# A planner that counts the delay of an engine's own last result, in a hybrid layer on one core

## The chip, the cores and the metric

The kernel runs on one core of a Trainium2 chip. Its time is the device time of one execution, in microseconds (us). The work is divided among five instruction streams, each of which runs in the order in which it was written: TensorE (PE) does the matmuls, VectorE (DVE), ScalarE (ACT) and GpSimd (POOL) the elementwise work, and SyncE (SP) issues the DMA transfers. An engine that meets an instruction whose input is not ready stands still, and all that is written behind that instruction waits with it.

## The reference

One layer over 1024 prompt tokens and 8 sample tokens, model width 1024, all in float32. Cut to what matters:

```python
xn   = rmsnorm(h, pre_g)
u, v, z_a, x_b, z_b, g_a, g_b = split(xn @ w_in)      # w_in: 1024 x 7168
u, vn = gelu(u), layernorm(gelu(v))
y_a  = u * (tril(w_s) mixes each 128-token chunk of vn, + b_s) * silu(z_a)
y_b  = blockdiag_linear(mean over 2/4/8/16 trailing rows of x_b, - x_b) * scale * silu(z_b)
m    = sigmoid(g_a) * (y_a @ w_pa) + sigmoid(g_b) * (y_b @ w_pb)
h    = h + rmsnorm(m @ w_out, post_g)
e    = p @ w_ple
h    = h + rmsnorm(sigmoid(rmsnorm(h, ple_in_g) @ w_pg) * e, ple_out_g)
```

The outputs are h for the prompt and the samples, the last chunk of vn, and the pooling rows (the last 15 rows of x_b, and for the samples the state shifted by one).

## The kernel before, in words

**Products.** Each float32 operand is cut into a high and a low part of the matmul type float32r, and a product is three matmuls (high by high, high by low, low by high). The high part is a copy on ACT (`xbw<-xbs`), the low part a subtraction on DVE (`xbw<-xbs,xbw`). Each large product is made by seven block products instead of eight (Strassen), so that sums and differences of blocks have to be made on DVE: of weight blocks (`xbs<-big`, `wgraw<-wgraw`), of token blocks (`big<-big`), and of results in PSUM (`acc<-acc,w`, `one<-acc,w`). The names of the PSUM banks are `acc00`, `acc01`, `acc10`, `acc11`, `one0`, `one1` (the views of the profile leave the digits out), and two more are used in turn for the rest (`q`, `mix`, `accm`, `sps`, `state`). There are 6013 matmuls, of 512 columns (`one`) or 260 (`acc`) for the most part.

**Stages.** The stages follow each other on PE: `p @ w_ple` with the first blocks of v; v; g_a with the mixing of the chunks; u and z_a in pairs of block products; x_b and z_b with the pooling; g_b; the two products with w_pa and w_pb; w_out; and at the end the gate w_pg. Between the stages tensors are parked in DRAM: `ya<-za` is the store of y_a rows, `big<-ya` their way back, `big<-mix` the way back of the mixed chunks, `wg<-wgraw` the parking of scaled columns of w_pg, `wolow<-big` that of block sums of w_out. `big` is the operand of the running stage and also the place where weights land (`big<-in_w_in_dram`). Everything else in SBUF lies in 46 equal slots, which are given to tensors one after the other (`SLOTS`), so that a tensor's first writer also waits for the last user of its slot.

**What sets the order.** The code does not write the order of the work. Every operation is recorded by the class `Planner` as an `Op`, with its readers and writers, and when all are recorded `Planner.order` simulates the five streams with durations out of a small model (`duration`), and at each step issues the operation that can start first; among those that can start at the same time the one with the smallest due time (`late`, counted back from the matmuls that need it, shifted by `PUSH`). When an operation's end is known, its successors get the time from which they can start (`ready`): on another engine that is the end plus `SEEN`, on the same engine the end itself. The list that comes out is written to the engines by `play`; all instructions carry therefore one line number, L408. The planner's times are used for nothing else: on the chip every instruction starts when its semaphores allow it. `order` also gives the slots, in the order of issue.

The constants that the change touches: `PUSH["out"]` and `PUSH["tok"]` move the due times of the work that takes a finished block product out of PSUM (`pushed("out" if form.tail else "tok", evacuate, p)`), `HASTE` is the number of microseconds within which the norms between w_out and the gate are to be done (`hasty`), and `TURNS` names for each pair of token blocks the steps at which the output norm (`out_finish`), the sum for the next norm (`gate_norm`) and the transposing of its result (`gate_input`) are recorded.

## Time and profile before

| | |
|---|---|
| median of 3 runs | 979.25 us (978.5 to 979.53) |
| the profiled execution | 978.55 us |
| its span, first to last instruction | 976.8 us |
| granted TensorE clock | 0.996 |
| PE busy | 960.1 us (98%), 6013 matmuls |
| DVE busy | 788.1 us (81%), 1326 instructions |
| ACT busy | 535.0 us (55%) |
| POOL busy | 76.8 us (8%) |
| DMA | 194.23 MB, mean 199 GB/s |

A row of the timeline has the start in us from the beginning of the span, the length, the engine, the line, the operation, out<-in by the program's names, the shapes, the count of instructions merged into it, and, where the engine stood idle before it, how long and what released it. Names have lost their numbers there: `za` may be any of za#0 to za#7. A row of the waits has the waiting instruction, what it waited for, the sum in us, how often, and the longest.

### The profile page before, as it was taken

The page shows a single profiled execution, that of the slowest core. Times are in us where ns is not written, and L with a number is a line of the kernel's source. Part 1 is how long each engine was busy: PE and PEld are TensorE (multiplying, and loading weights), DVE is VectorE, ACT ScalarE, POOL GpSimd, SP SyncE. Part 2 cuts the span into 40 slices and gives each one's busy share as a digit, 9 for nine tenths or more (in the row PEclk, how much of TensorE's full clock was granted, in tenths as well). Part 3 has the DMA queues.
Part 4 walks back from the last instruction along what each step waited for, and adds up shares of the span by engine and source line. Part 5 has one row for each costly group of instructions (what it writes and reads, how often), then busy time and mean ns, then how long its engine had stood idle before and what let it go on. Part 6 is the DMA issues. An engine that isn't in the chain of part 4 may idle for free.

```text
span 976.8 us, 16155 instructions
## 1 busy us (share of the span) xinstructions
PE 960.1 (98%) x6013; PEld 852.2 (87%) x6013; DVE 788.1 (81%) x1326; ACT 535.0 (55%) x1041; POOL 76.8 (8%) x117
## 2 busy tenths in 40 slices
PE   9999999999999999999999999999999999999995
PEld 7889999999998899899999999999999987688765
DVE  6998559988587978879698986596599789699957
ACT  7765457767444554344455443572363284688744
POOL 3200000000000000001011200000000001221203
PEclk9999999999999999999999999999999999999998
DMA  9524975554358945654344485793573276699795
GB/s 339 178 87 86 192 180 186 158 176 130 109 202 257 327 162 198 227 161 143 119 162 138 152 287 198 276 335 105 193 285 113 108 280 196 159 306 345 202 324 175
DMA packets 137982, 194.23 MB, mean 199 GB/s; under 512 B 42407, under 2 KB 93647, under 8 KB 137894
## 3 DMA queue, kind: packets, MB, share of 16 engines
q1 hardware_dynamic: 135853, 185.82, 57.4%
q0 software_dynamic: 2048, 7.37, 4.2%
q8 instruction: 47, 0.77, 0.3%
q14 instruction: 34, 0.27, 0.1%
HBM read 133.46 MB, written 60.16 MB: 198 GB/s over the span
## 4 chain that ended last, share of the span: by engine, by line
PE 88%; DMA 5%; DVE 4%; issue 1%; ACT 1%; POOL 1%; SPq 0%; POOLq 0%; DVEq 0%; ACTq 0%
PE acc L408 47%; PE one L408 36%; PE mix L408 1%; DVE big L408 1%; PE accm L408 1%; PE sps L408 1%; DVE za L408 1%; DMA big<-in_w_in_dram 1%; DMA wgraw<-in_w_pg_dram 1%; DMA big<-in_state_pool_dram 1%; DVE ge L408 1%; DMA weraw<-in_w_ple_dram 1%; POOL rstd L408 1%; DMA big<-in_w_out_dram 1%; DMA wohigh<-big 1%
## 5 line engine op out<-in xcount | busy, mean ns | idle before, releaser
L408 POOL TENSOR_TENSOR rstd<-ms,mhalf 128x1 f32<-128x1 f32 (+1 forms) x37 | 33.9, 928 | 504.2 <-DVE ms L408 475.1
L408 DVE TENSOR_TENSOR big<-big 128x512 f32<-128x512 f32 (+7 forms) x80 | 58.6, 741 | 4.7 <-DMA big<-in_w_in_dram 2.4
L408 DVE TENSOR_TENSOR one<-acc,w 128x260 f32<-128x260 f32 (+1 forms) x68 | 29.3, 431 | 21.6 <-PE acc L408 17.5
L408 ACT ACTIVATE qh<-big 128x512 fp32r<-128x512 f32 (+2 forms) x32 | 21.8, 696 | 30.5 <-DVE big L408 23.6
L408 ACT ACTIVATE acc<-one 128x260 f32<-128x260 f32 x66 | 21.3, 366 | 30.7 <-PE one L408 30.7
L408 ACT ACTIVATE w<-acc 128x260 f32<-128x260 f32 (+1 forms) x66 | 25.1, 410 | 21.5 <-PE acc L408 21.3
L408 DVE TENSOR_TENSOR ql<-big,qh 128x512 fp32r<-128x512 f32 (+2 forms) x32 | 24.3, 771 | 9.5 <-PE one L408 3.5
L408 POOL COPY big<-xb 128x1 f32<-128x1 f32 x8 | 4.5, 558 | 260.4 <-DMA yalow<-za 188.9
L408 ACT ACTIVATE gbw<-gbs 128x512 fp32r<-128x512 f32 x16 | 10.0, 628 | 21.1 <-DVE gbs L408 15.3
L408 ACT ACTIVATE pbw<-pbs 128x512 fp32r<-128x512 f32 x16 | 9.9, 627 | 18.1 <-DVE pbs L408 14.2
L408 DVE TENSOR_TENSOR gbw<-gbs,gbw 128x512 fp32r<-128x512 f32 x16 | 11.0, 687 | 10.9 <-ACT gbw L408 10.9
L408 ACT ACTIVATE paw<-pas 128x512 fp32r<-128x512 f32 x16 | 10.0, 628 | 13.3 <-DVE pas L408 11.2
L408 POOL COPY big<-big 128x2 f32<-128x2 f32 (+2 forms) x12 | 12.6, 1048 | 53.4 <-DVE big L408 39.1
L408 ACT ACTIVATE big<-mix 128x256 f32<-128x256 f32 x32 | 12.0, 382 | 8.4 <-PE mix L408 7.9
L408 ACT ACTIVATE junk<-h 128x512 bf16<-128x512 f32 x20 | 12.6, 630 | 6.6 <-DMA h<-in_x_prompt_dram 3.8
L408 ACT ACTIVATE vw<-vs 128x512 fp32r<-128x512 f32 x16 | 10.0, 626 | 10.6 <-DVE vs L408 7.9
L408 PE MATMUL mix<-wst,vh 128*128 128x256 f32 x64 | 15.6, 319 | 0.0
L408 DVE TENSOR_TENSOR za<-za,big 128x1024 f32<-128x1024 f32 (+2 forms) x16 | 15.2, 956 | 0.2
L408 ACT ACTIVATE junk<-ge 128x512 bf16<-128x512 f32 (+2 forms) x19 | 11.5, 603 | 6.9 <-DVE ge L408 6.1
L408 DVE TENSOR_TENSOR za<-za,u 128x1032 f32<-128x1032 f32 x8 | 9.8, 1229 | 6.3 <-ACT za L408 6.3
L408 ACT ACTIVATE acc<-none 128x8 f32<-128x8 f32 x33 | 5.9, 179 | 16.3 <-DVE big L408 7.8
L408 ACT ACT_TABLE_LOAD x11 | 14.1, 1283 | 1.0 <-PEq L2133 0.8
(712 smaller groups left out, 3635.1 us busy)
## 6 DMA issues: line engine op xcount, KB each, us to landing
big<-in_w_in_dram SPq DMA_DIRECT2D x48, 512.0 KB
ga<-ga SPq DMA_DIRECT2D x16, 516.0 KB
gb<-gb SPq DMA_DIRECT2D x16, 516.0 KB
ya<-za SPq DMA_DIRECT2D x8, 516.0 KB
yb<-zb SPq DMA_DIRECT2D x8, 516.0 KB
x<-in_x_prompt_dram SPq DMA_DIRECT2D x8, 512.0 KB
vraw<-in_w_in_dram SPq DMA_DIRECT2D x8, 512.0 KB
e<-e SPq DMA_DIRECT2D x8, 512.0 KB
```

Of the source, the lines that this page charges most:

```text
L408: getattr(getattr(self.nc, e), method)(*(self.real(a) for a in args), **{k: self.real(a) for k, a in kwargs.items()})
```

## The change

The planner's `order` adds a delay also where a successor is on the same engine: 0.12 us on DVE, 0.14 on ACT, 0.12 on POOL, 0 on PE. Its model of PE gets dearer for short matmuls (none under 0.109 us instead of 0.06, and 0.13 for those into `sps`, the sums of the sample rows). Four constants are set anew. No operation is added or taken away: each engine gets the same instructions, with the same operands, in another order, and many tensors lie in other slots (172 of 873 keep theirs).

```diff
-PUSH = {..., 'out': 3.0, 'sub': 3.0, 'tok': 1.0}
+PUSH = {..., 'out': 2.0, 'sub': 3.0, 'tok': 1.5}
...
-HASTE = 8.0
-TURNS = ((6, 8, 15), (14, 15, 18), (20, 28, 30), (27, 32, 36))
+HASTE = 2.0
+TURNS = ((6, 8, 13), (14, 15, 18), (20, 28, 30), (27, 32, 36))
...
     SEEN = {"tensor": 0.25, "vector": 0.15, "scalar": 0.20, "gpsimd": 0.20}
+    OWN = {"tensor": 0.0, "vector": 0.12, "scalar": 0.14, "gpsimd": 0.12}
...
-            return 0.109 if method == "transpose" else max(0.06, 0.0062 + n / 2268)
+            if out.tensor.name.startswith("sps"):
+                return 0.13
+            return 0.109 if method == "transpose" else max(0.109, 0.0062 + n / 2268)
...
-                a.ready = max(a.ready, end if o.moved or a.engine == e else end + self.SEEN[e])
+                a.ready = max(a.ready, end if o.moved else end + (self.OWN if a.engine == e else self.SEEN)[e])
```

Of the 1326 instructions of DVE 334 stand at another place (by up to 58), of ACT 170 (up to 39), of the 689 groups of matmuls on PE 11 (by up to 2), of SP's 465 transfers 39 (up to 10). The first 60 us are the same on all of them. Three places follow, which the prediction speaks of. A row has the line, the operation, the tensors and the size of the output; the line of the changed kernel is L411.

DVE at 74 to 81 us, before. `v_1237<-acc_74` and `v_1237<-acc_75` are the two additions that take a finished product out of the banks acc10 and acc11.

```order
L408 TENSOR_TENSOR vs_1126<-vs_1126,vraw_478 128x512
L408 TENSOR_TENSOR big<-big 128x1024 x2
L408 TENSOR_TENSOR vw_1186<-vs_1126,vw_1186 128x512
L408 TENSOR_TENSOR vw_1165<-vraw_457,vw_1165 128x512
L408 TENSOR_TENSOR vw_1199<-vraw_463,vw_1199 128x512
L408 TENSOR_TENSOR vs_1126<-vraw_480,vs_1126 128x512
L408 TENSOR_TENSOR v_1237<-acc_74,u_712 128x260
L408 TENSOR_TENSOR v_1237<-acc_75,u_712 128x260
```

The same place in the changed kernel (where the tensor's name is `v_1202`):

```order
L411 TENSOR_TENSOR big<-big 128x1024
L411 TENSOR_TENSOR vs_1129<-vs_1129,vraw_478 128x512
L411 TENSOR_TENSOR v_1202<-acc_74,u_712 128x260
L411 TENSOR_TENSOR v_1202<-acc_75,u_712 128x260
L411 TENSOR_TENSOR big<-big 128x1024
L411 TENSOR_TENSOR vw_1206<-vs_1129,vw_1206 128x512
L411 TENSOR_TENSOR vw_1164<-vraw_457,vw_1164 128x512
```

The two additions stand five places earlier, ahead of one of the long token-block sums and of four other subtractions.

ACT at 322 to 329 us, before. The three copies `acc00`, `acc01` and `acc11` put starting values into banks that PE goes on adding to; `zaw_420` is the high part of a weight block for z_a, which is given the slot of y_a rows that the transfer `ya<-za` has to have read first.

```order
L408 ACTIVATE u_412_3727<-u_412_3727 128x520
L408 ACTIVATE acc00_72<-one0_76 128x260
L408 ACTIVATE acc01_73<-one0_76 128x252
L408 ACTIVATE acc11_75<-acc10_74 128x260
L408 ACTIVATE zaw_420_3823<-big_104 128x512
L408 ACTIVATE zaw_423_3859<-zas_419_3651 128x512
```

The same place in the changed kernel:

```order
L411 ACTIVATE u_412_3728<-u_412_3728 128x520
L411 ACTIVATE zaw_420_3802<-big_104 128x512
L411 ACTIVATE acc00_72<-one0_76 128x260
L411 ACTIVATE acc01_73<-one0_76 128x252
L411 ACTIVATE acc11_75<-acc10_74 128x260
L411 ACTIVATE zaw_423_3858<-zas_419_3653 128x512
```

The copy `zaw_420` has moved from behind the three copies to ahead of them; its slot is the same in both kernels.

DVE at the end of the kernel, before. `ms_428` is the mean square of the last block of tokens, from which POOL makes the last `rstd_429`; the `SCALAR_TENSOR_TENSOR` rows scale a block of the output and add h.

```order
L408 TENSOR_TENSOR ge_9991<-ge_9991,out_9397 128x256
L408 SCALAR_TENSOR_TENSOR ge_10022<-ge_10022,rstd_423,hback_9983 128x512
L408 TENSOR_SCALAR ms_428<-ssq_426,sofar_427 128x1
L408 SCALAR_TENSOR_TENSOR ge_10022<-ge_10022,rstd_423,hback_9983 128x512
L408 TENSOR_TENSOR ge_9991<-ge_9991,out_9397 128x256
L408 SCALAR_TENSOR_TENSOR ge_9991<-ge_9991,rstd_429,hback_9997 128x512 x2
```

The same place in the changed kernel:

```order
L411 TENSOR_TENSOR ge_10000<-ge_10000,out_9396 128x256
L411 SCALAR_TENSOR_TENSOR ge_10028<-ge_10028,rstd_423,hback_9981 128x512 x2
L411 TENSOR_SCALAR ms_428<-ssq_426,sofar_427 128x1
L411 TENSOR_TENSOR ge_10000<-ge_10000,out_9396 128x256
L411 SCALAR_TENSOR_TENSOR ge_10000<-ge_10000,rstd_429,hback_9997 128x512 x2
```

The mean square has moved behind the second half of the block before it.

Elsewhere, in words. Between 375 and 405 us DVE does the two block differences `xbs` (of weights for x_b) after the low part of `zaw#23` instead of before the sums ahead of it, and the long product `za#7 * u#10` comes ahead of the low part of `xbw#0`; on PE twelve matmuls `one1<-xbw#0` come ahead of six `acc10<-qh#8`, and the eight `state` matmuls ahead of the first three of `acc00<-xbw#5`. On SP the store `wg<-wgraw#1` is put behind `big<-mix` and `ya<-za#2` (at 318 us); the load `wpool#0` (at 418 us) is given a slot that is read by matmuls ending at 428 us; and the loads `wgraw#2` to `wgraw#5` come behind weight loads that they preceded.

## The prediction

> **What bounds the kernel now.** I read the page first, then the waits of PE, then the timelines of the places that these name. The page:

> ```profile
> PE 960.1 (98%) x6013; PEld 852.2 (87%) x6013; DVE 788.1 (81%) x1326; ACT 535.0 (55%) x1041; POOL 76.8 (8%) x117
> PE 88%; DMA 5%; DVE 4%; issue 1%; ACT 1%; POOL 1%; SPq 0%; POOLq 0%; DVEq 0%; ACTq 0%
> ```

> PE is busy for 960.1 of 976.8 us and makes up 88% of the chain. The change gives PE the same matmuls, so that it can win only what PE loses in waits, and at both ends. The first 60 us stay as they are. The table by stage, and the waits of PE:

> ```profile
> 300.00:400.00 100.00, 96.67 (x629) 87.25 (x627) 85.49 (x138) 50.10 (x101) 0.00 (x0) 1.00 0.73 237
> 960.00:977.00 17.00, 5.95 (x39) 5.22 (x38) 12.13 (x28) 6.17 (x18) 5.15 (x4) 0.78 0.68 196
> ...
> PE q L408 <- DVE ql L408: 1.3, 1, 1.3
> PE state L408 <- DMA big<-in_state_pool_dram: 0.7, 1, 0.7
> PE one L408 <- DVE zaw L408: 0.7, 1, 0.7
> ```

> (Columns of the table: length, busy time of PE, PEld, DVE, ACT and POOL, clock, DMA share, GB/s.) From 300 to 400 us PE loses 3.3 us, and from 960 on it has 6 us of work in 17. With one of 0.74 at 79.49 us (below) these waits make up 3.4 us. Each is a little dearer than its row:

> ```profile
> 324.07 0.29 PE L408 MATMUL q<-secondh,qh 128*128 128x260 f32 x1
> 324.20 0.28 PE L408 MATMUL q<-secondl,qh 128*128 128x260 f32 x1
> 325.80 0.39 PE L408 MATMUL q<-secondh,ql 128*128 128x260 f32 x1 [1.32 <-DVE ql L408]
> ```

> A matmul of 0.29 us is followed by the next 0.13 us after its own start (324.07, 324.20) where nothing holds it; 1.60 us passed here, so that about 1.48 are lost for an idle time of 1.32. I add 0.16 to each wait: 0.90 at 79.5 us, 1.48 at 325.8, 0.82 at 337.3, 0.88 at 399.4. About 4.1 us, 0.4% of the time, is nearly all that a better order can win.

> **The change part by part.** Each sum is made against the profiled execution of 978.55 us (span 976.8 and 1.75 around it), 0.7 below the median.

> *At 79.5 us.* The wait's name says ACT, but these are the rows:

> ```profile
> 77.71 1.04 PE L408 MATMUL psw<-ident,ws 128*128 128x128 f32 x8
> 79.49 0.36 PE L408 MATMUL acc<-xB22h,vw 128*128 128x260 f32 x1 [0.74 <-ACT wst L408]
> 74.24 2.35 DVE L408 TENSOR_TENSOR big<-big 128x1024 f32<-128x1024 f32 x2
> 77.12 1.28 DVE L408 TENSOR_TENSOR vw<-vraw,vw 128x512 fp32r<-128x512 f32 x2
> 78.93 0.75 DVE L408 TENSOR_TENSOR v<-acc,u 128x260 f32<-128x260 f32 x2
> ```

> PE needs bank acc10, and DVE empties it from 78.93 on. These two additions now stand ahead of one `big` sum (1.2 us) and four subtractions (four times 0.61 to 0.69 of DVE's time): 3.9 us earlier. PE finds the bank empty: **-0.90**. The displaced work is late by the 0.75 us of the additions, and PE does not wait for it within 3 us. If something else holds PE there, 0.

> *100 to 300 us and the banks at 428 us.* DVE's order is drawn anew most densely in the mixing of the chunks, but moves by about 2 us in places with 2 us in hand. The nearest place:

> ```profile
> 194.15 0.68 DVE L408 TENSOR_TENSOR gaw<-gas,gaw 128x512 fp32r<-128x512 f32 x1
> 205.95 0.28 PE L408 MATMUL acc<-xT1h,gaw 128*128 128x260 f32 x1
> ```

> The low part of this block is moved 22 places back, 11.6 us by the rows that lie between, and had 11.1 us in hand; PE asks for it with its second or third matmul, 0.2 us later. The copies into the banks at 428 us move back 1.06 us with 0.88 in hand. For these together **+0.2**, between 0 and +0.9.

> *312 to 326 us.* ACT and SP:

> ```profile
> 323.18 0.65 ACT L408 ACTIVATE acc<-one 128x260 f32<-128x260 f32 x2 [0.28 <-PE one L408]
> 325.91 0.64 ACT L408 ACTIVATE zaw<-big 128x512 fp32r<-128x512 f32 x1 [1.65 <-DMA ya<-za]
> 317.86 0.33 SPq L408 DMA_DIRECT2D wg<-wgraw  x1
> 318.71 0.79 SPq L408 DMA_DIRECT2D ya<-za  x1
> 318.00:326.00 8.00, 6.24 (x38) 5.30 (x38) 7.55 (x14) 5.95 (x14) 0.00 (x0) 1.00 0.96 318
> ```

> Two things happen. DVE brings `ql#7` forward: two `wgraw` subtractions go behind it, a long `big` comes ahead, and block sums that depend on each other are interleaved with others. Dependent sums start 0.03 us after the end of the last (the rows here), independent ones 0.08 before it (969.30 and 969.97 in the rows of the end, below):

> ```profile
> 331.90 0.69 DVE L408 TENSOR_TENSOR us<-big 128x512 f32<-128x512 f32 x1
> 332.62 0.69 DVE L408 TENSOR_TENSOR us<-us,big 128x512 f32<-128x512 f32 x1
> ```

> Some six pairs win 0.11 us each, so that `ql#7` ends at about 325.0 instead of 325.74: 0.74 of the 1.48 us. But on ACT the copy `zaw#14`, which waits until the store `ya<-za#2` has read its slot (325.91 before, 7.2 us after the issue), now stands ahead of the copies into acc00, acc01 and acc11 (323.18), which PE needs at 323.7. The store issues about 2.5 us earlier, since DVE makes `za#2` in an idle time, and is no longer behind the store of `wg`. The DMA engines are full in these 8 us (share 0.96, 318 GB/s), so that I give it only what leaves the queue ahead of it: 0.52 MB at 318 GB/s, 1.65 us. It lands at 324.3; `zaw#14` ends at 324.9, the first bank is filled at 325.2, and the matmul that came at 325.80 comes at 325.95: **+0.15**. Bounds: landed by 323, -0.74; landed at 325.91 as before, the banks are filled at 326.85 and that matmul comes at 327.6, +1.8.

> [...]

> *336 us.* The wait for `zaw#16`:

> ```profile
> 335.07 0.63 ACT L408 ACTIVATE zaw<-big 128x512 fp32r<-128x512 f32 x1 [5.32 <-DMA ya<-za]
> 333.75 2.87 DVE L408 TENSOR_TENSOR big<-big 128x512 f32<-128x512 f32 x4 [0.43 <-DMA big<-in_w_out_dram]
> 336.54 0.68 DVE L408 TENSOR_TENSOR zaw<-big,zaw 128x512 fp32r<-128x512 f32 x1
> ```

> Its low part stands behind four sums (2.87 us) and now ahead of them. It then waits for its high part (335.70, itself behind a store that issues about 1.3 us earlier), and ends by 336.4 at the latest; PE asks at 336.46. **-0.82**, at worst 0.

> *375 to 402 us.*

> ```profile
> 379.53 0.28 PE L408 MATMUL acc<-xB22l,zaw 128*128 128x260 f32 x1
> 379.89 0.51 PE L408 MATMUL acc<-xB22h,zaw 128*128 128x260 f32 x2
> 382.58 0.69 DVE L408 TENSOR_TENSOR xbw<-big,xbw 128x512 fp32r<-128x512 f32 x1 [2.41 <-ACT xbw L408]
> 386.19 1.23 DVE L408 TENSOR_TENSOR za<-za,u 128x1032 f32<-128x1032 f32 x1
> 392.91 0.35 SPq L408 DMA_DIRECT2D big<-in_state_pool_dram  x1
> 399.40 1.95 PE L408 MATMUL state<-mask,big 120*128 120x8 f32 x16 [0.72 <-DMA big<-in_state_pool_dram]
> ```

> `zaw#23` gets another slot, whose last user is done 2 us earlier, and its two parts come earlier by about as much: the 0.24 us lost between 379.53 and 379.89 go, **-0.24**. Then the low part of `xbw#0` falls behind `za#7 * u#10` (1.23), while PE wants it 0.7 us earlier, at about 382.9. ACT is ahead by the same 1 to 2 us, so that it ends at 382.6 if the earlier work moves up, and at 383.9 if not: between 0 and +1.0, **+0.2**. The `state` matmuls wait for a load that landed at 399.4, 6.5 us after its issue, and it goes behind DVE's multiplication of `za#7`, which I put 0.4 us later. Three loads in its way issue 1.6 us earlier, since DVE reads their places earlier. Landing is thus between 398.4 and 399.8. In the new order nothing stands before `state` to fill the wait (three matmuls, 0.36): from -0.65 to +0.75, **-0.2**.

> *The end.*

> ```profile
> 969.30 0.75 DVE L408 SCALAR_TENSOR_TENSOR ge<-ge,rstd,hback 128x512 f32<-128x512 f32 x1
> 969.97 0.21 DVE L408 TENSOR_SCALAR ms<-ssq,sofar 128x1 f32<-128x1 f32 x1
> 970.10 0.74 DVE L408 SCALAR_TENSOR_TENSOR ge<-ge,rstd,hback 128x512 f32<-128x512 f32 x1
> 970.26 0.98 POOL L408 TENSOR_TENSOR rstd<-ms,mhalf 128x1 f32<-128x1 f32 x1 [0.99 <-DVE ms L408]
> 971.28 1.41 DVE L408 SCALAR_TENSOR_TENSOR ge<-ge,rstd,hback 128x512 f32<-128x512 f32 x2
> ```

> `ms` now stands behind the second of the long operations, which starts 0.67 us after the first (969.30 and 969.97). POOL, the last two operations of DVE and the last transfers all come 0.67 us later; nothing else runs. **+0.67**, the surest term.

> The sum: -0.90 + 0.2 + 0.15 - 0.82 - 0.24 + 0.2 - 0.2 + 0.67 = -0.94. That makes 977.6 for the profiled execution and **978.3 for the median**. About 0.2%, 1.96 us, can be told from no change by a measurement of this kernel, so that this counts as the same.

> **The rivals.**

> *Transfers come early.* If the three transfers land near their lower bounds, the sum is 0.89, 0.45 and 0.2 us less: -2.5, **976.8**. For it: each issues 1 to 2.5 us earlier. Against it: the engines' share of 0.96.

> *Transfers land no earlier, and ACT waits ahead of the banks.* At 323.7 us the order bets on a store. If the engines have to move the same bytes by then, it lands at 325.9: +1.8 instead of +0.15; all behind it on ACT and DVE is late, the next store with it, and the wait for `zaw#16` stays (+0.82); the load of `state` is late too (+0.75 instead of -0.2). That is +3.4 us on the sum, **981.7**, slower. It decides from a landing of about 324.9, where this place loses 0.75. For it: the share of 0.96, and the second store, no larger, for which ACT waits 5.32 us. Against it: the store does pass 0.52 MB.

> *SP stands behind a slot.* `wpool#0` was loaded at 417.71, used by ACT at 429.81 and by PE at 434.45:

> ```profile
> 417.71 0.38 SPq L408 DMA_DIRECT2D wpool<-in_w_pool_dram  x1
> 429.81 0.63 ACT L408 ACTIVATE wpoolw<-wpool 128x512 fp32r<-128x512 f32 x1
> ```

> Its slot is free only at 428.3 now. With 7.2 us, as the slowest store above, it lands at 435.5, PE waits until 436.8: +2.35, 980.7. With up to 4.8 us it costs nothing.

> *The change does nothing to the waits*, since the planner's clock isn't the chip's: the terms cancel, 979.25.

> **How the numbers follow.** Forecast 978.3: 0.35. Early transfers: 0.27. Late transfers: 0.20. SP's slot: 0.06. Nothing: 0.12. Faster by over 0.2% (below 977.3) is the first rival and 0.05 of the forecast, 0.32; slower (above 981.2) the second, 0.20; the rest 0.48. The range goes from 976.5, the first rival with 0.3 less, to 981.8, the second; the forecast's own is 977.2 to 979.8.

> **What would show it.** PE's wait at 79.5 us is gone; so is that for `zaw`. Before 326 us PE waits for ACT's `acc<-one`, and that for the store; if it waits for `ql` alone, the store was early. The last `ms` starts 0.67 us after the start of the first of the two long operations behind it before, and the end of PE to the end of the span is 0.7 us longer. A wait of over 1 us between 400 and 960 us, where PE has none now, would make the whole account wrong.

## The result, and the profile after

| | before | after |
|---|---|---|
| median | 978.88 us of 4 (978.29 to 979.53) | 973.48 us of 4 (973.29 to 973.95) |
| ratio | | 0.9945, 95% interval 0.9928 to 0.9963 |
| the profiled execution | 978.55 us | 973.95 us |
| its span | 976.8 us | 972.0 us |
| start of the last matmul | 965.67 us | 960.71 us |

The change makes the kernel 5.4 us faster. The prediction had 0.9 us, and 976.5 to 981.8 us as its range; 973.5 us lies outside it. Beside the later runs the kernel before had medians of 979.9 to 980.4 us (15 to 29 executions each), and the changed kernel once more 973.0 us, so that 5.4 us, from four executions of each, is rather the low end of the gain. The page of the changed kernel (busy times, and the chain by engine):

```profile
PE 956.6 (98%) x6013; PEld 851.4 (88%) x6013; DVE 780.9 (80%) x1326; ACT 533.0 (55%) x1041; POOL 80.2 (8%) x117
PE 93%; DMA 3%; DVE 1%; ACT 1%; issue 1%; POOL 0%; SPq 0%; POOLq 0%; DVEq 0%; ACTq 0%
```

PE is busy for 3.5 us less with the same matmuls. The row of a matmul is longer than the step to the next (0.28 us, and 0.13 apart), so that a hold of up to 0.15 us counts as busy time and not as a wait, and a matmul that was held is itself shown as longer (0.36 to 0.50 us in place of 0.28 to 0.40); fewer were held (at full clock and behind the first 20 us, 48 rows of matmuls of 260 or 512 columns are 0.03 us or more longer than the others of their size, in the kernel before 51). Of the 3.5 us 0.8 lie in the first 20 us, where PE stands for loads instead. PE's share of the chain rises from 88% to 93%. The waits of PE, all of them, in the changed kernel:

```profile
PE warm L411 <- DVE heat L411: 1.5, 1, 1.5
PE acc L411 <- ACT wehi L411: 1.5, 1, 1.5
PE acc L411 <- ACT acc L411: 0.7, 1, 0.7
PE vecs L411 <- DMA vecs<-in_ple_in_g_dram: 0.5, 1, 0.5
PE pp L411 <- DMA p<-in_p_prompt_dram: 0.2, 1, 0.2
```

Behind the first 16 us, where both programs are the same and loads from DRAM set the pace (6.2 us of `weraw` and 7.3 us of `vecs` in the chain), one wait is left: 0.7 us for ACT's copies into the banks. (A second profile of the same kernel, after2, has 0.9 us of further waits for DVE and ACT between 875 and 895 us.) The table by stage, with the columns of before:

```profile
300.00:400.00 100.00, 99.32 (x662) 91.24 (x661) 86.02 (x146) 49.98 (x102) 0.00 (x0) 1.00 0.74 248
955.00:972.00 17.00, 5.99 (x40) 5.25 (x38) 12.04 (x28) 5.33 (x14) 5.51 (x5) 0.77 0.69 195
```

From 300 to 400 us PE now loses 0.7 us (before: 3.3), and the end is nearly as long as it was.

Where the time went can be read without any model: the same matmul's start in the two profiled executions, after minus before, as PE goes on.

| place | predicted | difference gained there |
|---|---|---|
| up to 20 us (same program) | 0 | +1.1 (this execution's loads; another execution of the same kernel began 1.0 earlier) |
| 79.5 us | -0.90 | -0.99 |
| 100 to 300 us, and the banks at 428 us | +0.2 | -0.15 |
| 312 to 326 us | +0.15 | -1.65 |
| 336 us | -0.82 | -0.91 |
| `zaw#23` at 379.5 us | -0.24 | -0.31 |
| `xbw#0` and `state`, to 402 us | 0.0 | -1.1 |
| 402 to 966 us | 0 | -0.84 (not repeated in after2, which loses 1.5 us between 870 and 895) |
| behind PE | +0.67 | +0.15 |

Four rows make up nearly all of the miss: 312 to 326 us (1.8), `state` (1.1), 402 to 966 us (0.8) and the end (0.5). The start lost 1.1 us, so that behind the first 20 us the profile won 6.0 us (after2: 4.7). The first of the four is in these rows, PE before and then PE after:

```profile
316.57 0.35 PE L408 MATMUL acc<-xB22h,uw 128*128 128x260 f32 x1
320.10 0.50 PE L408 MATMUL one<-xB11h,zaw 128*128 128x512 f32 x1 [0.44 <-ACT u L408]
323.69 0.30 PE L408 MATMUL acc<-xT2h,zaw 128*128 128x260 f32 x1
```

```profile
316.18 0.28 PE L411 MATMUL acc<-xB22h,uw 128*128 128x260 f32 x1
319.06 0.40 PE L411 MATMUL one<-xB11h,zaw 128*128 128x512 f32 x1
323.39 0.39 PE L411 MATMUL acc<-xT2h,zaw 128*128 128x260 f32 x1 [0.68 <-ACT acc L411]
324.11 0.28 PE L411 MATMUL q<-secondh,ql 128*128 128x260 f32 x1
```

The differences are -0.39, -1.04, -0.30 and, with 325.80 of before, -1.69. So 1.0 us was won ahead of the bank copies, on two waits that the prediction did not count; the copies themselves took 0.7 back, as it said; and then the wait for `ql#7` went whole.

### The profile page after: what moved, and what is told of

It reads as the page before. It is cut to its first block, busy times and chain, and to the rows that moved or that the text cites. A ratio compares the mean times of both kernels' runs of the same rounds, so it can differ in the third digit from the quotient of the medians.

```text
span 972.0 us, 16134 instructions
## 1 busy us (share of the span) xinstructions
PE 956.6 (98%) x6013; PEld 851.4 (88%) x6013; DVE 780.9 (80%) x1326; ACT 533.0 (55%) x1041; POOL 80.2 (8%) x117
## 4 chain that ended last, share of the span: by engine, by line
PE 93%; DMA 3%; DVE 1%; ACT 1%; issue 1%; POOL 0%; SPq 0%; POOLq 0%; DVEq 0%; ACTq 0%
PE acc L411 50%; PE one L411 39%; PE mix L411 1%; PE accm L411 1%; PE sps L411 1%; DVE ge L411 1%; DMA vecs<-in_ple_in_g_dram 1%; DMA big<-in_w_in_dram 1%; DMA wgraw<-in_w_pg_dram 1%; DMA weraw<-in_w_ple_dram 1%; PE q L411 1%; POOL rstd L411 0%; DVE big L411 0%; ACT junk L411 0%; PE pst L411 0%
## 5 line engine op out<-in xcount | busy, mean ns | idle before, releaser
L411 POOL TENSOR_TENSOR rstd<-ms,mhalf 128x1 f32<-128x1 f32 (+1 forms) x37 | 35.4, 969 | 500.8 <-DVE ms L411 492.3
L411 DVE TENSOR_TENSOR big<-big 128x512 f32<-128x512 f32 (+7 forms) x80 | 58.4, 739 | 1.9 <-DMA big<-in_w_out_dram 0.9
L411 DVE TENSOR_TENSOR one<-acc,w 128x260 f32<-128x260 f32 (+1 forms) x68 | 29.3, 430 | 22.3 <-PE acc L411 19.3
L411 ACT ACTIVATE w<-acc 128x260 f32<-128x260 f32 (+1 forms) x66 | 25.4, 412 | 27.6 <-PE acc L411 26.1
L411 ACT ACTIVATE acc<-one 128x260 f32<-128x260 f32 x66 | 21.3, 366 | 32.7 <-PE one L411 32.5
L411 DVE TENSOR_TENSOR ql<-big,qh 128x512 fp32r<-128x512 f32 (+2 forms) x32 | 24.1, 772 | 10.5 <-ACT qh L411 4.2
L411 ACT ACTIVATE qh<-big 128x512 fp32r<-128x512 f32 (+2 forms) x32 | 22.0, 696 | 17.1 <-DVE big L411 8.5
L411 POOL COPY big<-xb 128x1 f32<-128x1 f32 x8 | 4.5, 564 | 257.4 <-DMA yalow<-big 183.5
L411 ACT ACTIVATE pbw<-pbs 128x512 fp32r<-128x512 f32 x16 | 9.9, 627 | 19.5 <-DVE pbs L411 16.2
L411 ACT ACTIVATE gbw<-gbs 128x512 fp32r<-128x512 f32 x16 | 9.9, 628 | 16.9 <-DVE gbs L411 8.2
L411 DVE TENSOR_TENSOR gbw<-gbs,gbw 128x512 fp32r<-128x512 f32 x16 | 11.0, 688 | 9.9 <-ACT gbw L411 9.8
L411 ACT ACTIVATE big<-mix 128x256 f32<-128x256 f32 x32 | 12.1, 383 | 10.3 <-PE mix L411 9.8
L411 DVE TENSOR_TENSOR hw<-hs,hw 128x512 fp32r<-128x512 f32 x16 | 11.0, 685 | 8.1 <-ACT hw L411 8.1
L411 ACT ACTIVATE paw<-pas 128x512 fp32r<-128x512 f32 x16 | 9.9, 627 | 13.4 <-DVE pas L411 13.2
L411 PE MATMUL mix<-wst,vh 128*128 128x256 f32 x64 | 15.6, 319 | 0.0
L411 DVE TENSOR_TENSOR za<-za,big 128x1024 f32<-128x1024 f32 (+2 forms) x16 | 15.3, 955 | 0.1
L411 ACT ACTIVATE mw<-ms 128x512 fp32r<-128x512 f32 x16 | 9.9, 627 | 9.4 <-DVE ms L411 8.3
L411 DVE TENSOR_TENSOR gaw<-gas,gaw 128x512 fp32r<-128x512 f32 x16 | 10.9, 683 | 4.8 <-ACT gaw L411 4.7
L411 ACT ACTIVATE acc<-none 128x8 f32<-128x8 f32 x33 | 6.0, 183 | 15.7 <-DVE gb L411 7.7
L411 DVE TENSOR_TENSOR big<-mix,big 128x256 f32<-128x256 f32 x32 | 12.8, 418 | 2.1 <-ACT big L411 1.8
L411 PE MATMUL mix<-wst,vl 128*128 128x128 f32 x64 | 14.2, 223 | 0.0
```

What stands on the lines that cost most here:

```text
L411: getattr(getattr(self.nc, e), method)(*(self.real(a) for a in args), **{k: self.real(a) for k, a in kwargs.items()})
```

## The experiments

All were timed against the kernel before on the same chip. Three kinds of kernel are used. A *window* takes one program's list of instructions and draws those that begin in a stretch of time in the order of the other program:

```diff
-            for e, (method, args, kwargs) in self.order():
+            ordered = self.order()
+            for first, places in MOVED:
+                ordered[first : first + len(places)] = [ordered[p] for p in places]
+            for e, (method, args, kwargs) in ordered:
```

The slots stay those of the program whose list it is. A *move* uses the same lines for a few instructions. An *exchange* lets two tensors, and all that follow them in their slots, change places:

```diff
+SWAPS = ((37, 12, 20, 11),)
...
+            for a, i, b, j in SWAPS:
+                ua, ub = ([n for n in self.place if self.place[n] == s][k:] for s, k in ((a, i), (b, j)))
+                self.place.update({**{n: b for n in ua}, **{n: a for n in ub}})
```

### Which part of the change: own_only, consts_only, no_own

```diff
 own_only:    + OWN and its use in order(); nothing else
 consts_only: + PUSH out 2.0, tok 1.5; HASTE 2.0; TURNS (6, 8, 13); nothing else
 no_own:      the changed kernel with OWN = 0.0 for all engines
```

> The kernel before with the delay for an engine's own last result (OWN) alone; the model of short matmuls and the four constants as before. In its list of instructions DVE's v#4, ql#7, the wgraw subtractions and ACT's zaw#13 and zaw#14 stand where they stood before. Theory: the delay gave none of the gains at 79.5 and 312 to 326 us, whose waits stay (0.7, 0.3, 0.6 and 1.3 us): ratio 0.999 to 1.000. Rival: what the change gains is the overlap of interleaved operations on DVE and ACT all along the program, by which everything there is early; then at least half of the 5.4 us is seen, 0.997 or less, with the waits at 316 to 326 us shorter.

> The kernel before with the four constants alone (PUSH out and tok, HASTE, TURNS). v#4 stands where it stood before, the place at 312 to 326 us is as without OWN: zaw#13 early, ql#7 ahead, bank copies ahead of zaw#14. Theory: the wait at 79.5 us stays (0.74), those at 316 to 337 us go: 0.9 us less gain than with the model of short matmuls beside it, ratio 0.9955 if that one is 0.9945. Rival: the constants move the norms at the end only, and the gain at 312 us is chance of the slots: 0.999.

> The changed kernel with OWN set to zero: the model of short matmuls and the four constants alone. Here v#4 stands early, zaw#13 ahead of wgraw on ACT, ql#7 ahead of the wgraw subtractions, and the three bank copies ahead of zaw#14 again. Theory: all of the gain at 79.5 and 312 to 326 us is here, and 0.7 us more, since the wait behind zaw#14 is not: ratio 0.9945 or a little less (0.994). Rival (the overlap of interleaved work): at most half of the gain, 0.997 or more.

Measured: own_only 0.9994 (0.9983 to 1.0005), consts_only 0.9985 (0.9975 to 0.9996), no_own 0.9977 (0.9965 to 0.9989). No part comes near the whole; own_only and no_own together would give 0.9971, where the whole gave 0.9945 and later 0.992.

My theory about own_only fell in its rows, though its ratio came out. `v#4` and `ql#7` stand at the very places of before, yet PE's waits for them are gone:

```profile
77.81 0.60 PE L409 MATMUL psw<-ident,ws 128*128 128x128 f32 x4
78.25 0.36 PE L409 MATMUL acc<-xB22h,vw 128*128 128x260 f32 x1
...
880.66 0.48 PE L409 MATMUL one<-woB22h,mw 128*128 128x512 f32 x1 [0.65 <-DVE h L409]
895.38 0.50 PE L409 MATMUL one<-wgT1h,hw 128*128 128x512 f32 x1 [0.45 <-DVE one L409]
```

Against the same matmuls of before, 0.90 is won at 79.5 us, 1.17 at 325.8 and 0.59 at 337.3. DVE does its 1326 operations in less time: 780.8 us in all, where before has 788.1. It is so wherever the list is made with OWN (780.7 to 781.9 us in ten profiles, a window of the other order in it or not), and nowhere else (786.4 to 788.1 in ten): the overlap of interleaved work is real (in the profile after, 992 of the operations start ahead of the end of the one before them, in the profile of before 920, in both by 0.08 us in the median). What is won is lost again at 205 to 216 us (0.8), at the bank copies of 323.7 us (0.5), behind the load of `state` (1.4, see the clock below), and at 880 to 900 us (2.2), where the waits quoted are new. The changed kernel has waits at the same places in after2, so that the last loss need not be this order's.

In consts_only the wait at 79.5 us stays (0.88 us), as expected, and 312 to 337 us give 2.2 us; 1.0 us goes back at 392.8 us. no_own has both gains and stands 0.9 us behind the changed kernel at 402 us (both counted from 20 us); its profile then loses 5 us at 938 us:

```profile
934.54 1.03 PE L411 MATMUL sps<-wgrow,sst 128*8 128x512 f32 x4
938.07 1.04 PE L411 MATMUL sps<-wgrow,sst 128*8 128x512 f32 x4 [2.49 <-DMA wgrow<-wg]
939.04 0.80 PE L411 MATMUL one<-wgT4h,hw 128*128 128x512 f32 x1
939.63 0.63 PE L411 MATMUL one<-wgT4l,hw 128*128 128x512 f32 x1
```

2.7 us are the late transfer; 1.5 us are the clock, which for one stretch of 3.4 us makes a matmul of 0.23 us from start to start into one of 0.43; the rest is lost among the `sps` matmuls themselves. So the constants and the model of short matmuls give most of what is won up to 340 us, and the delay (OWN) mainly keeps it from being given back. That is read from one profile each; the times say only that all parts are needed. The model of short matmuls was not run alone.

### Which place: t60, t300, u300, t365, u365, t900

Windows: t60 (60 to 100 us), t300 (296 to 345), t365 (360 to 408) and t900 (845 to the end) are the kernel before with one stretch in the changed order; u300 and u365 are the changed kernel with one stretch in the order of before.

> The kernel before with one stretch of its list of instructions, those that begin between 60 and 100 us, drawn in the order of the changed kernel; the slots of before and all else stay. Prediction (its first term): PE finds the banks acc10 and acc11 empty at 79.5 us, -0.90 us, and nothing else changes: ratio 0.9991. Rival: the 0.9 us are given back at the next late transfer, because PE comes earlier to waits whose ends are set by DMA: 0, ratio 1.000. The rows of the changed kernel show -0.99 at this matmul and no change up to 300 us.

> The kernel before with the stretch from 296 to 345 us alone in the order of the changed kernel (on all engines, SP too; slots of before). Prediction: +0.15 at 312-326 us and -0.82 at 336 us, together -0.67, ratio 0.9993. Theory now, from the rows of the changed kernel: the high part of zaw#13 stands ahead of the waits for qh#6 and wgraw on ACT, so that za#2 is multiplied and stored 4.6 us earlier, and ACT waits neither for the load of wgraw#1 nor for the store: -1.75 and -0.92, together -2.7, ratio 0.9973. Rival: the two gains need the other slots or the earlier PE of the changed kernel; then under 1.2 us are seen here.

> The changed kernel with the stretch from 296 to 345 us back in the order of the kernel before (slots of the changed kernel). If the order there is what gave 2.7 us, they are lost: the waits for ql#7 (1.3) and zaw (0.7) are back, and 0.9973 results; if ACT, DVE and SP are then late behind it as before, the gain of 0.9 us at the load of state goes too: 0.998. By the prediction this stretch is worth 0.67: 0.9952.

> The kernel before with the stretch from 360 to 408 us alone in the order of the changed kernel; slots of before. Prediction: -0.24 at zaw#23 (by another slot, so 0 here with the slot of before), +0.2 at xbw#0, -0.2 at the load of state: together 0.0 to -0.24, ratio 0.9998 to 1.000. From the rows of the changed kernel: -0.35, 0 and -0.91, together -1.26, ratio 0.9987. Rival: the load of state came earlier only because all of SP's transfers ahead of it did (gains at 312-337 us); then the wait for state stays here, and -0.3 at most is seen.

> The changed kernel with the stretch from 360 to 408 us back in the order of the kernel before (slots of the changed kernel). The rows of the changed kernel have -0.35 at zaw#23 and -0.91 at the load of state. Theory: the state load comes early because the order at 312-337 us makes everything ahead of it early, not because of the order here; then at most 0.4 us is lost, 0.9949. Rival: the state matmuls' own order and SP's order here gave it; then 1.26 us are lost, 0.9958.

> The kernel before with the stretch from 845 us to the end alone in the order of the changed kernel; slots of before. Prediction: +0.67 us, since the last ms stands behind the second long operation: ratio 1.0007. From the rows of the changed kernel: PE gains 0.35 us between 900 and 950 us and the end behind PE is 0.15 longer: -0.2, ratio 0.9998. Rival: POOL's last rstd took 0.66 us in place of 0.98 and the last store 3.66 in place of 4.11 by chance of that execution; then +0.3 to +0.4 here.

| | ratio, 95% | against its own parent, by the same matmuls |
|---|---|---|
| t60 | 0.9989 (0.9976 to 1.0002) | -0.99 at 79.5 us |
| t300 | 0.9988 (0.9976 to 1.0000) | -1.42 from 312 to 340 us, +1.27 at 378 us |
| u300 | 0.9955 (0.9940 to 0.9970) | +2.93 from 312 to 340 us |
| t365 | 0.9995 (0.9981 to 1.0008) | +1.35 from 382 to 393 us, the wait for `state` gone, then some 1.5 by the clock |
| u365 | 0.9941 (0.9921 to 0.9962) | +1.31 at 383 us |
| t900 | 1.0150 (1.0132 to 1.0169) | +13.5 from 700 us to the end |

The first term of the prediction holds by itself: t60 wins 0.99 us at the very matmul (its time alone could not tell this: 1.0 lies within the interval). u300 settles the largest miss: with the order of 296 to 345 us undone, the changed kernel loses 2.93 us there (time: 975.89 us, where the changed kernel has 973.0 to 973.5), and all the waits of before are back, in these rows and at `zaw` (0.6 us):

```profile
315.80 0.36 PE L417 MATMUL acc<-xB22h,uw 128*128 128x260 f32 x1 [0.70 <-DVE u L417]
319.12 0.50 PE L417 MATMUL one<-xB11h,zaw 128*128 128x512 f32 x1 [0.20 <-ACT u L417]
324.82 0.39 PE L417 MATMUL q<-secondh,ql 128*128 128x260 f32 x1 [1.33 <-DVE ql L417]
```

The same order put into the kernel before (t300) wins half of that and gives most of it back 40 us later, where PE, now earlier, waits for DVE and ACT. u365 is the other side of this: without the changed order at 360 to 408 us, the changed kernel waits there too:

```profile
384.41 0.39 PE L417 MATMUL acc<-xT2h,xbw 128*128 128x260 f32 x1 [1.04 <-ACT acc L417]
```

So the order at 375 to 402 us wins little by itself, but without it 1.3 of the 2.9 us would be given back. My expectation for t365 from the rows of the changed kernel (-1.26) was wrong for that reason; the wait for `state` goes in it because PE comes 1.35 us later. For u365 the loss has the size of the rival (1.26), but another cause: it is at `xbw`, and the load of `state` is no wait in it, as the theory had it. t900 says nothing of the last term: that order in the slots of before makes PE wait 3.6 us for DVE's `one` and 2.9 for ACT's `wgB21h`. An order and its slots belong together.

### The loads at 302 to 316 us: t300s, a_slot, b_slot

t300s is t300 with an exchange of `wgraw#0` and `uw#15`, a_slot the changed kernel with an exchange of `wgraw#0` and `uw#16`, b_slot the kernel before with the exchange of t300s alone.

> The kernel before with the stretch from 296 to 345 us in the order of the changed kernel, and with one exchange of slots: from this place on, wgraw#0 and uw#15 take each other's slot, so that the eight loads of wgraw no longer wait for DVE's product za#2*u#5 but, as in the changed kernel, for matmuls with uw#12. Theory: the stretch alone gave only about 1.2 us because the loads of wgraw began 1.7 us later behind that product; with the exchange the load of wgraw#1 ends before 316 us (relative to PE as in the changed kernel), the wait for u at 320 us goes, and the two stretches give -2.7: ratio 0.9973. Rival: the load ends late because the DMA engines are full whatever the slot; then as the stretch alone, 0.9988, and PE still waits about 0.9 us for u.

> The changed kernel with one exchange of slots: wgraw#0 and uw#16 take each other's slot from 300 us on, so that the loads of wgraw wait for DVE's product za#2*u#5, as in the kernel before. Theory (slot): the load of wgraw#1 lands 1 to 1.7 us later, ACT's u and its copies come later by as much, PE loses about 1.2 us at 320 to 324 us against the changed kernel: ratio to the kernel before 0.9957 instead of 0.9945. Rival (the order alone): no change against the changed kernel, 0.9945.

> The kernel before with the exchange of slots alone (wgraw#0 and uw#15 take each other's slot from 302 us on; no instruction is moved). Theory (load): in the kernel before the eight loads of wgraw are issued 1.0 us behind the weight load from which DVE makes the sum for qh#6, and take the DMA engines from it; in its profile that load lands just in time, in another execution (b_state) DVE stood 2.84 us for it and PE lost 2.5 us at 316 us. In the changed kernel the gap is 2.4 us and DVE never stands there. With the other slot the first load of wgraw waits for matmuls with uw#12, about 0.8 us longer: DVE's wait goes, the loads of wgraw end no later, and the median is 0.5 to 1.5 us lower (0.9985 to 0.9995) with times closer together. Rival: wgraw lands later by the same 0.8 us, ACT stands longer at it, and PE loses 0.5 to 0.8 us more at 320 us: 1.0005 to 1.001.

t300s: 0.9985 (0.9969 to 1.0001). In its rows 312 to 340 us give 2.80 us in place of t300's 1.42, as the theory has it; but `uw#15` is late now (+0.73 ahead of 312 us), 1.29 go back at 378 us and 0.79 at 880 us. a_slot: 0.9923 (0.9905 to 0.9941), no slower than the changed kernel; of the 1.2 us expected 0.39 is in the rows. b_slot: 1.0010 (0.9997 to 1.0022), no gain. The slot of `wgraw#0` thus matters in the kernel before with the new order, and hardly in the changed kernel, where the product that it waits for is done early. Neither exchange is the cause of the result.

What is early in the changed kernel are these rows of ACT and DVE:

```profile
309.49 0.63 ACT L411 ACTIVATE zaw<-zas 128x512 fp32r<-128x512 f32 x1 [3.05 <-DVE zas L411]
315.50 1.15 ACT L411 ACTIVATE wgraw<-wgraw,gvec 128x1024 f32<-128x1024 f32 x1 [3.15 <-DMA wgraw<-in_w_pg_dram]
...
322.43 0.64 ACT L411 ACTIVATE zaw<-big 128x512 fp32r<-128x512 f32 x1
```

```profile
311.71 0.69 DVE L411 TENSOR_TENSOR zaw<-zas,zaw 128x512 fp32r<-128x512 f32 x1
312.31 1.22 DVE L411 TENSOR_TENSOR za<-za,big 128x1024 f32<-128x1024 f32 x1
```

In the kernel before these were:

```profile
312.06 1.15 ACT L408 ACTIVATE wgraw<-wgraw,gvec 128x1024 f32<-128x1024 f32 x1 [1.14 <-DMA wgraw<-in_w_pg_dram]
313.12 0.61 ACT L408 ACTIVATE zaw<-zas 128x512 fp32r<-128x512 f32 x1
316.68 1.15 ACT L408 ACTIVATE wgraw<-wgraw,gvec 128x1024 f32<-128x1024 f32 x1 [2.95 <-DMA wgraw<-in_w_pg_dram]
...
316.67 1.22 DVE L408 TENSOR_TENSOR za<-za,big 128x1024 f32<-128x1024 f32 x1
```

ACT makes the high part of `zaw#13` at 309.49 us, ahead of the first `wgraw`; before, it did so at 313.12 us, behind it. DVE, which waited for it, multiplies `za#2` at 312.31 us (before 316.67), and SP's store of it is issued at 314.10 us (before 318.71). When ACT comes to `zaw#14`, whose slot the store reads, there is nothing to wait for. ACT's second `wgraw` comes 1.2 us earlier too (315.50, before 316.68), and with it the gelu for which PE waited at 320.10 us. This chain is read from the rows: u300 undoes the order of the whole stretch, and no run moves `zaw#13` alone.

### The load of state, and the clock: after2, a_state, b_state, a_dense

after2 is the changed kernel once more. The others are moves: a_state puts four DVE operations ahead of `za#7 * big`; b_state (kernel before) puts DVE's last layernorm and `za#7 * big` each ahead of one copy; a_dense (changed kernel) puts one `state` matmul behind every three of the 24 that follow.

> The changed kernel again, beside the three that follow. Theory (clock): the gain has a part that no wait shows. In the kernel before PE stands for 0.7 us at the load of state and then does 16 matmuls of 8 columns in 1.95 us; in several profiles of such kernels the granted clock then is 0.50 for 3.4 us (1.6 us lost), in others not. In the changed kernel that wait is gone, and no profile of it shows the clock below 1.00 at this place: its times lie within 2 us of each other where those of the kernel before lie over 6, and the median is 0.993 to 0.9945 of before. Rival: the spread of the kernel before is the chip's own, and the changed kernel spreads as wide here.

> The changed kernel with four DVE operations (2.3 us) moved ahead of the product za#7 * big, behind which the load of state is issued. The load lands 2.3 us later; PE waits 1.0 to 2.3 us for it. Theory (clock): this and the 1.85 us of small matmuls make a thin stretch of over 3 us, after which the clock is 0.50 for 3.4 us in at least half of the executions: 2 to 4 us more than the changed kernel, and times that fall in two groups 1.6 us apart. Rival: the wait alone is lost, 1.0 to 2.3 us, and the clock stays 1.00.

> The kernel before with two DVE operations each moved ahead of one copy of 0.4 us (the layernorm of the last mixed chunk and the product za#7 * big), so that the load of state is issued 0.67 us earlier. The prediction's term for this load had the bound -0.65. Theory: PE's wait of 0.72 us goes, 0.7 to 0.9 us; with it the dips of the clock behind it become rarer, and the median falls by 0.9 to 1.6 us, ratio 0.9983 to 0.9990, with fewer executions over 981 us. Rival: only the wait goes, 0.9991, and the spread stays.

> The changed kernel with the eight state matmuls (16 instructions of 8 columns, 1.85 us with little work in them) spread among the 24 matmuls that follow, one after every three. Theory (clock): no thin stretch is left, so that no execution has the dip; since the changed kernel has it rarely, if at all, the median stays within 0.3 us of the changed kernel, unless the loading of the small matmuls' weights (0.19 us each) is hidden behind the larger matmuls, which would save up to 1 us. Rival: the interleaved weight loads hold PE, and up to 1.5 us are lost.

| | ratio, 95% | times |
|---|---|---|
| after2 | 0.9920 (0.9906 to 0.9935) | 972.35 to 974.30 us |
| a_state | 0.9958 (0.9943 to 0.9973) | 975.83 to 979.00 us |
| b_state | 1.0000 (0.9984 to 1.0016) | 977.63 to 984.94 us |
| a_dense | 0.9924 (0.9911 to 0.9938) | 972.59 to 973.97 us |

The wait by itself can be made and is dear. In a_state PE stands for 2.08 us, and then its matmuls take twice as long (PE, then the table by stage, whose last columns are granted clock, DMA share and GB/s):

```profile
395.64 2.18 PE L417 MATMUL state<-mask,big 120*128 120x8 f32 x16 [2.08 <-DMA big<-in_state_pool_dram]
397.67 0.57 PE L417 MATMUL acc<-xB22h,xbw 128*128 128x260 f32 x1
...
394.00:396.00 2.00, 0.36 (x4) 0.36 (x4) 1.67 (x5) 1.01 (x3) 0.00 (x0) 1.00 0.44 142
396.00:398.00 2.00, 2.00 (x16) 2.00 (x16) 0.14 (x1) 0.33 (x1) 0.00 (x0) 0.80 0.42 171
398.00:400.00 2.00, 2.00 (x11) 2.00 (x11) 0.76 (x3) 0.00 (x0) 0.00 (x0) 0.50 0.52 213
```

2.24 us are the wait and 1.6 the clock, together 3.9; the median is 3.6 us above after2. The same happens behind shorter waits. In t60, where this place is as before:

```profile
399.52 1.95 PE L414 MATMUL state<-mask,big 120*128 120x8 f32 x16 [0.88 <-DMA big<-in_state_pool_dram]
...
398.50:401.92 3.42, 2.54 (x23) 2.40 (x22) 3.38 (x9) 2.07 (x4) 0.00 (x0) 1.00 0.02 6
401.92:405.33 3.41, 3.41 (x19) 3.41 (x18) 0.59 (x1) 0.00 (x0) 0.00 (x0) 0.50 0.38 155
405.33:408.74 3.41, 3.41 (x19) 2.89 (x19) 2.67 (x5) 1.16 (x5) 0.00 (x0) 1.00 0.28 109
```

Of the profiles with a wait of 0.6 us or more at `state`, t60, t900, b_slot, own_only and a_state have this dip behind it, and the profile of before that the prediction was made from does not. Of the others only t365 has it, where PE stands for some 0.3 us ahead of the small matmuls. No profile of the changed kernel or of its variants without that wait does.

Which execution is hit can be read from the record of the granted clock. In all 20 profiles the clock changes only on a grid of 3.413 us, counted from where the record of full clock begins (4.5 to 7.3 us into the span, at another point in each), and each dip ahead of the end fills one window of this grid. In the profile of before the record of full clock lasts 962.56 us, 282 such steps, and in that of after 959.15 us, 281. In t60 a window begins at 398.50 us and holds the thin stretch whole (rows above). In the profile of before a window begins at 399.33 us, inside the stretch, and both of its parts pass:

```profile
395.92:399.33 3.41, 2.76 (x14) 2.10 (x12) 3.38 (x8) 1.73 (x4) 0.00 (x0) 1.00 0.62 126
399.33:402.74 3.41, 3.34 (x29) 3.34 (x30) 3.17 (x8) 1.28 (x3) 0.00 (x0) 1.00 0.21 86
```

Counted in columns of matmuls from the rows (an estimate), the windows just ahead of the ten dips have at most some 2800, out of about 7500 in a full one, and no other window at full clock, ahead of the end, has under some 3250. The changed kernel's 16 small matmuls leave about 3700 even where one window holds them all (394.06 to 397.47 us in its profile). What looks like chance is thus where the grid lies. If it can lie anywhere, the 2.7 us thin stretch of before (398.51 to 401.20) is hit in some three of five executions, an estimate from these figures.

So the `state` term of the prediction (-0.2, between -0.65 and +0.75) missed twice: the wait went whole (0.88 us at that matmul), and in the kernel before it draws a further 1.6 us in some executions, by the estimate above in more than half. b_state was to show this in the times: the wait is gone in its rows (-0.69), but 0.6 us are lost ahead of it at the copies that were put back, and its median is that of before, with a spread as wide. The interval reaches from -1.6 to +1.6 us. In the same profile something else struck, at 316 us, where b_state's program is still that of before:

```profile
311.69 0.69 DVE L414 TENSOR_TENSOR big<-big 128x512 f32<-128x512 f32 x1 [2.84 <-DMA big<-in_w_in_dram]
...
318.44 0.35 PE L414 MATMUL acc<-xB22h,uw 128*128 128x260 f32 x1 [2.58 <-DVE u L414]
...
320.00:322.00 2.00, 2.00 (x11) 2.00 (x10) 1.77 (x5) 1.97 (x4) 0.00 (x0) 0.50 0.84 295
```

DVE stood 2.84 us for a weight load, PE lost 2.5 us to it, and then the clock fell to 0.50 here as well. Against the profile of before, the stretch from 312 to 318 us took 0.62 us longer in t60, 0.46 in t365, 1.39 in t900 and 2.56 in b_state, all with the program of before there; among seven profiles of the changed kernel and its variants in which that stretch is the changed one, none differs by 0.01 us. The kernel before has thus two places where its executions differ, by up to 2.6 us, and the profiles of the changed kernel differ at neither. That these two make up its whole spread is not shown. 110 executions of it beside these runs (two of over 1100 us left out) are between 977.3 and 984.3 us, half of them between 979.2 and 981.3; 27 of the changed kernel and of the variants a_ms, a_slot and a_dense are between 972.2 and 974.9. a_dense has no thin stretch left and is neither faster nor slower than after2: in the changed kernel the small matmuls alone do no harm.

### The end, and all together: a_ms, best

```diff
 a_ms (DVE, the changed kernel)
   SCALAR_TENSOR_TENSOR ge_10028<-ge_10028,rstd_423,hback 128x512
+  TENSOR_SCALAR ms_428<-ssq_426,sofar_427 128x1
   SCALAR_TENSOR_TENSOR ge_10028<-ge_10028,rstd_423,hback 128x512
-  TENSOR_SCALAR ms_428<-ssq_426,sofar_427 128x1
```

best is the changed kernel with this move, the move of a_dense, the exchange of a_slot, and the three bank copies ahead of `zaw#14` on ACT.

> The changed kernel with one instruction moved: the last ms ahead of the second of the two long operations behind which it was put. By the prediction's last term POOL's rstd, the two last operations of DVE and the last stores all come 0.67 us earlier: 0.67 us less than the changed kernel, ratio 0.9938 where that one has 0.9945. By the traces (the end of PE to the end of the span grew by 0.15 only) 0.15, which cannot be told from nothing. The trace tells by the time from the end of the last accumulation of PE to the end of the span.

> The changed kernel with four small edits together: the three bank copies ahead of zaw#14 on ACT, the last ms ahead of the second long operation, the eight state matmuls spread among 24 others, and the exchange of slots between wgraw#0 and uw#16. By the rows: PE's wait of 0.7 us for the copies goes, but ql#7 ends 0.5 us later than the copies' users, so that about 0.2 to 0.5 is won there; up to 0.67 at the end (0.15 by the traces); the other two nothing by themselves. Together 0.4 to 1.2 us below the changed kernel: ratio 0.9908 to 0.9930 where that one has 0.992. Rival: all of it is hidden behind the next wait; no difference from the changed kernel.

a_ms: 0.9933 (0.9916 to 0.9949), between the two values of the changed kernel (0.9945 and 0.9920). DVE and POOL at the end of the changed kernel, and then of a_ms:

```profile
964.60 1.41 DVE L411 SCALAR_TENSOR_TENSOR ge<-ge,rstd,hback 128x512 f32<-128x512 f32 x2 [0.45 <-POOL rstd L411]
966.22 0.66 POOL L411 TENSOR_TENSOR rstd<-ms,mhalf 128x1 f32<-128x1 f32 x1 [1.65 <-DVE ms L411]
966.92 1.42 DVE L411 SCALAR_TENSOR_TENSOR ge<-ge,rstd,hback 128x512 f32<-128x512 f32 x2 [0.44 <-POOL rstd L411]
```

```profile
964.05 0.75 DVE L417 SCALAR_TENSOR_TENSOR ge<-ge,rstd,hback 128x512 f32<-128x512 f32 x1 [0.45 <-POOL rstd L417]
965.01 0.99 POOL L417 TENSOR_TENSOR rstd<-ms,mhalf 128x1 f32<-128x1 f32 x1 [0.99 <-DVE ms L417]
966.03 1.41 DVE L417 SCALAR_TENSOR_TENSOR ge<-ge,rstd,hback 128x512 f32<-128x512 f32 x2
```

With `ms` early, POOL's operation takes 0.99 us in place of 0.66 (0.98 in the kernel before, 0.66 again in after2), and the last two operations of DVE begin 1.98 us after the first of the block ahead, in place of 2.32: 0.34 of the 0.67 us is left. From the end of those two to the end of the span it is then 4.16 us (967.44 to 971.6) in place of 3.66 (968.34 to 972.0). The last stores take back the rest, and from PE's last matmul to the end of the span it is about 0.1 us longer with the early `ms` (11.41 us for 11.32). The "surest term" of the prediction is worth nothing.

best: 974.20 us, 0.9946 (0.9931 to 0.9961), no better than the changed kernel, which had 0.9945 and, on another chip, 0.9920 (after2). Its rows say why: the copies' wait shrinks from 0.68 to 0.19 us and `ql#7` takes 0.4 of that back, while the exchange of slots costs 0.74 us at 319 us, twice what it cost in a_slot. None of the kernels beats the change.

## Why the prediction was wrong, point by point

**What bounds the kernel** held in kind: what was won, PE had lost in holds. Its size did not. "About 4.1 us is nearly all that a better order can win" looks close to the 4.6 us by which the time of the profiled execution fell, but this is luck: that execution lost 1.1 us at its start, and 6.0 us were won behind it. The sum had left out the wait of 0.44 us at 320.10 us (its row stands in the result) and all holds of under 0.15 us, which no wait shows. The steps that turned 4.1 us into 0.9 us failed as well.

**79.5 us, 336 us, `zaw#23`:** -0.90, -0.82 and -0.24 came as -0.99, -0.91 and -0.31, and t60 has the first alone. **100 to 300 us:** +0.2 came as -0.15; nothing was late.

**312 to 326 us, +0.15:** this is the step that failed most. It put DVE's product `za#2` 2.5 us earlier and the store's landing at 324.3 us. The product was 4.4 us earlier and the store issued 4.6 us earlier, because ACT makes the high part of `zaw#13` ahead of the first `wgraw`, for whose load it stood 1.14 us before; that move was in the order and not in the sum. The landing, on which the bounds from -0.74 to +1.8 and the first two rivals rested, decided nothing: `zaw#14` found it done. `ql#7` was ready 1.9 us earlier (323.82 us, before 325.75) where the sum had 0.74, and PE's wait for it went whole. The copies behind `zaw#14` did cost 0.7 us, but not by the store: 0.5 of it is the time of `zaw#14` itself, as best shows, where the copies go first. The waits at 316.6 and 320.1 us were not in the list of what could be won at all. By u300 the order from 296 to 345 us is worth 2.9 us, where the prediction had 0.67.

**`xbw#0` and `state`, 0.0 together:** `xbw#0` came in time (0 for +0.2): by u365, the new order there is what prevents a wait of 1.0 us. The load of `state` landed before PE asked, beyond the lower bound of -0.65. The loads ahead of it were issued 4.7 us before it in place of 2.6 us, so that less was in its way (DMA share 0.76 in the 3 us behind its issue, before 1.01). The prediction had this reason, sized at 1.6 us, and still took the value nearest to no change.

**402 to 966 us, 0:** 0.84 us were won in small steps, 0.18 of them between 537 and 612 us, 0.26 between 800 and 900 and 0.36 at the sums of the sample rows (930 to 950 us). Since after2 loses 1.5 us between 870 and 895, this row differs from one execution to the next; its cause was not tried.

**The end, +0.67:** measured +0.15. The step that failed is that all behind `ms` moves by as much: POOL's operation is 0.32 us shorter there (0.66 for 0.98), and the stores behind take up the rest.

**The rivals.** The nearest to the result was the first, early transfers, with 976.8 us; it had the direction, and was too small by the waits not counted. Of the others none shows: PE has no wait between 400 and 960 us in the profile after, so SP's slot cost nothing, and the waits did change. The clock was in no part of the prediction: the granted clock of the one profile was 1.00 at `state`, and only the place of the grid in that execution kept it so.

**What stays open:** how often the clock dips in the kernel before, beyond the estimate, and how much of its spread that is; whether the move of `zaw#13` alone gives what u300 takes away; why the parts of the change do not add up in time (by their ratios own_only and no_own 2.8, the whole 5.4 to 7.8 us), beyond the places named; and the drift of 0.4 us between 400 and 900 us.

## What to carry to other kernels

In a new order, follow every engine that the bound engine waits for back through the moves ahead of the wait, and list each wait of the stage, however short, before sizing one: a copy put ahead of an instruction that stands for a transfer can bring a whole chain forward by more than the transfer's own change. A window of one order put into the other program gave less here than the same window took away from its own, since the neighbours and the slots that make use of the gain are missing; test a reordering by undoing it. Read the granted clock behind each wait of the matmul engine in several profiles: a wait of under 1 us beside small matmuls can cost more in the 3.4 us that follow than it shows (t60: 0.88 us of wait, then 3.4 us at a clock of 0.50), and one profile at full clock does not clear it.
